# A planner's prices for transposes, single-precision products and scans are set anew

## The chip, the cores and the metric

The kernel runs on one core of a Trainium2 chip. The metric is the device time of one execution in microseconds (us). PE is the matrix engine, PEld its weight loads, DVE the vector engine, ACT the scalar engine, SP the engine that issues most DMAs, POOL a general engine that does almost nothing here. PE accumulates into eight banks of PSUM; all other tiles lie in SBUF.

## The reference

A trunk of two layers on one sequence of 512 tokens with 1024 features, in float32. Each layer is a half-step SwiGLU feed-forward block, a mixer, and another feed-forward block, every one behind an RMSNorm and added to `x`; a last RMSNorm ends it.

```python
for i in range(DEPTH):                        # DEPTH = 2
    x = x + 0.5 * swiglu(rmsnorm(x, ffn1_norm[i]), ...)    # 1024 -> 2816 -> 1024
    h = rmsnorm(x, mix_norm[i])
    y = gla_mixer(h, ...) if i % 2 == 0 else sb_mixer(h, ...)
    x = x + y
    x = x + 0.5 * swiglu(rmsnorm(x, ffn2_norm[i]), ...)
return rmsnorm(x, final_norm)

# gla_mixer: four heads, q and k of 128, v of 256; b = cumulative log decay
scores[t, s] = sum_k q[t, k] * exp(b[t, k] - b[s, k]) * k[s, k]      # s <= t
state = exp(b_last) * state + (k * exp(b_last - b)).T @ v
o = rmsnorm(scores @ v + (q * exp(b)) @ state) * silu(g);  y = o @ w_out

# sb_mixer: sixteen heads of 64; mask is s < t
z = q @ k.T / 8
sp = where(mask, softplus(z), 0)
rem = reverse_cumsum(sp) - sp
w = where(mask, exp(log_sigmoid(z) - rem), 0);  y = (w @ v) @ w_out
```

## The kernel before

`x` is kept transposed, as eight tiles of 128 features by 512 tokens. Large products are made in three: weight and operand are each split into a high part, rounded by ACT (`wh`, `xh`, `oh`, a CAST), and a low part, the remainder that DVE takes (`wl`, `xl`, `ol`, a subtraction); PE then forms high by high, low by high and high by low (line 475, `mm`). Weights arrive by DMA in pieces of 128 by 1024 numbers (`raw`) and are split in lines 534 and 535. Work inside the mixers that is not a weight product stays in plain single precision on PE: transposes against `ident`, products of weights with values.

The program has six stages: feed-forward; the gated linear attention (GLA), about 343 to 547 us; feed-forward twice; the stick-breaking mixer (SB), about 1199 to 1422; feed-forward.

In GLA the heads follow one another; while PE projects for later parts (`ps_f`, `ps_t`), a head's output is formed. The names used below: `osq`, the squares of the head's output (ACT, DVE line 1641); `sh` and `sl`, the split of their sum (`sl` by DVE, line 1648); `ps_on`, two products that sum `sh` and `sl` over the features; `y`, the scale made of it (line 1658); `gn`, the gate (line 1413 to 1423); `kd`, the decayed keys of the next head (DVE lines 1580 and 1587), transposed on PE in line 1597 (`ps_kd`). `ps_s` is the update of the state (line 1607).

In SB a step `s` treats one of the 16 heads in three groups of query blocks. The logits `ps_z` come from PE (line 1815, `kh`, `kl` and `mq` being the split keys and queries, `negm` the causal mask, which may be put in ahead and then opens the bank). ACT makes `l` = log(1 + exp(-abs z)) and `r` = relu(z) of it (lines 1857, 1032, 1860); DVE scans `l` + `r` backwards along the keys (line 1863, four scans a head of 512, 384, 256 and 128 numbers a partition), and subtracts the result from `ps_z` (line 1871), which frees the bank. A step later PE transposes that (`ps_T`, line 1885), ACT takes exp of it (`wt`, line 1032), and PE multiplies with the values for a pair of heads (`ps_oT`, line 1900), which is split into `oh` and `ol` (lines 1909, 1910). Beside it run the projections of the next heads (`ps_f`, evacuated as `n` by DVE in lines 1774 and 1792, then split and laid out by ACT and DVE in lines 1782 to 1802), and at the end of the stage the output projection (`ps_b`).

What order these instructions have on each engine is not that of the program's text. The program is written down once in an order; then `Planner` reads all its instructions and their dependences (`gather`), gives each a price in nanoseconds (`price`: when its result is there, `cost`, and for PE how long the engine is taken, `step`), works back from PE's instructions in the order of the text when each other instruction is due (`due`, `late`), and plays the program through (`run`). PE takes the first instruction of the text, among the next sixty open ones, that could start by now; the others take, of what is ready, the one due earliest, and may wait a little for one that is more urgent. SP goes by due times too. The resulting order of each engine's queue is then fixed. So a price is never a time on the chip: it changes which instruction stands ahead of which in a queue, and the semaphores between the engines stay.

The classes of price are told by the instruction's types and shapes. A scan was to be told by the name of the instruction's class:

```python
if "Scan" in kind:
    n *= 2
elif len(reads) == 1 and not psum_in and n > 256:
```

In this program the scan of line 1863 is an instruction of the class of SCALAR_TENSOR_TENSOR, so the first branch was never taken.

Of the kernel before, what the change touches and what calls it, by code (L numbers as in the profile page):

```python
# [19 lines left out]
P = 128  # L20
# [15 lines left out]
def spots(dims):  # L36

    m = 1
    for step, n in reversed(dims):
        if step == 1 and m == 1:  # L40
            m = (1 << n) - 1
        elif step:
            one = m
            for i in range(1, n):
                m |= one << (i * step)
    return m


class Planner:
# [31 lines left out]
    def gather(self):  # L81
        self.eng, self.ins, self.succ, self.pred, self.after, self.tiles = [], [], [], [], [], []
        self.held, self.cost, self.step = [], [], []
        tag = {t.name: str(t.cap_key() if callable(t.cap_key) else t.cap_key) for t in self.tc.info.tiles}
        pools = {p.id: p for p in self.tc.info.pools}
        self.bufs, self.pool_of = {}, {}
        for c in set(tag.values()):
            nm, _, pid = c.rsplit("_", 2)
            self.bufs[c] = pools[int(pid)].tag_meta[nm].bufs or 1
            self.pool_of[c] = int(pid)  # L90
        self.tag, self.users, self.first, self.index = tag, {}, {}, {}
        live, last_pe, bounds, masks = {}, {}, [], {}
        for i in self.bb.instructions:
            kind = type(i).__name__
            if kind.startswith("BassTile"):
                if kind == "BassTilePoolBoundary":
                    bounds.append((i.name, str(i.op), len(self.eng)))
                continue
            e = str(i.engine).split(".")[-1]
            k = self.index[i.name] = self.node(e, i)  # L100
            sizes, psum_in, wide = [], False, 0
            for write, refs in ((False, i.ins), (True, i.outs)):
                for r in refs:
                    b = getattr(r, "bass_ap", None)
                    if b is None:
                        continue
                    ap = [(int(s), int(n)) for s, n in b.ap]
                    n = 1
                    for _, c in ap[1:]:
                        n *= c  # L110
                    sizes.append((write, n, str(r.dtype), ap[0][1]))
                    t = b.tensor
                    if type(t).__name__ != "Tile" or t.name not in tag:
                        continue
                    bank = "pp" in tag[t.name].rsplit("_", 2)[1]
                    psum_in |= bank and not write
                    free = 1
                    for d in t.shape[1:]:
                        free *= int(d)
                    if bank:  # L120
                        m = 1
                    else:
                        key = (free, int(b.offset), tuple(ap))
                        m = masks.get(key)
                        if m is None:
                            at = int(b.offset) + sum(s * (n - 1) for s, n in ap[1:] if s < 0)
                            one = spots([(abs(s), n) for s, n in ap[1:]]) << (at % free)
                            p0, m = at // free // 32, 0
                            for q in range(p0, p0 + (ap[0][1] + 31) // 32):
                                m |= one << (q * free)  # L130
                            masks[key] = m
                    if t.name not in self.first:
                        self.first[t.name] = k
                        self.users[t.name] = []
                        live[t.name] = ([], [])
                    if not self.users[t.name] or self.users[t.name][-1] != k:
                        self.users[t.name].append(k)
                        self.tiles[k].append(t.name)
                    writes, reads = live[t.name]
                    for x, mx in writes:  # L140
                        if x != k and mx & m and not (bank and e == "PE" == self.eng[x]):
                            self.edge(x, k)
                    if write:
                        for x, mx in reads:
                            if x != k and mx & m:
                                self.edge(x, k)
                        writes[:] = [(x, mx & ~m) for x, mx in writes if mx & ~m] + [(k, m)]
                        reads[:] = [(x, mx & ~m) for x, mx in reads if x == k or mx & ~m]
                        if bank and e == "PE":
                            if last_pe.get(t.name, k) != k:  # L150
                                self.order(last_pe[t.name], k)
                            last_pe[t.name] = k
                    else:
                        if bank:
                            for x, _ in reads:
                                if x != k and self.eng[x] != e:
                                    self.edge(x, k)
                        reads.append((k, m))
            self.cost[k], self.step[k] = self.price(i, kind, e, sizes, psum_in)
        self.n_ins = len(self.eng)  # L160
        for a, b in self.behind_:
            self.order(self.index[a], self.index[b])
        self.seq = {}
        for t in sorted(self.first, key=lambda t: (self.first[t], int(t.rsplit("_", 1)[1]))):
            self.seq.setdefault(tag[t], []).append(t)
        self.place = {t: j for l in self.seq.values() for j, t in enumerate(l)}
        self.at = [float(k) for k in range(self.n_ins)]
        self.stack(bounds, pools)
        self.tables()

    def price(self, i, kind, e, sizes, psum_in):
        n = max((s[1] for s in sizes), default=1)
        if e == "PE":
            types = [s[2] for s in sizes]
            if any("bfloat16" in t for t in types):
                return 270.0, max(64.0, 0.43 * n)
            if any("float32r" in t for t in types):
                return 165.0 + 0.42 * n, max(112.0, 0.422 * n)
            moving = sizes[0][1]
            full = sizes[1][1] == P and not kind.endswith("Transpose") and not getattr(i, "is_transpose", False)  # L180
            return 150.0 + 0.9 * n, max(58.0, 0.845 * moving) * (2 if full and moving in (1, P) else 1)
        if "DMA" in kind:
            total = max((s[1] * s[3] for s in sizes), default=1) * 4
            return 2050.0 + total / 318.0, total / 318.0
        scalars = sum(1 for s in sizes[:-1] if s[1] == 1 and n > 1)
        if e == "DVE":
            reads = [s for s in sizes[:-1] if s[1] > 1]
            if "Scan" in kind:
                n *= 2
            elif len(reads) == 1 and not psum_in and n > 256:  # L190
                n *= 0.5
            return 148.0 + 1.045 * n + 60.0 * scalars, 0.0
        if e == "Activation":
            if "Load" in kind:
                return 1290.0, 0.0
            return 190.0 + 0.835 * n + 95.0 * scalars - 30.0 * psum_in, 0.0
        return 200.0 + n, 0.0
# [2129 lines left out]
```

## Time and profile before

| | us |
|---|---|
| median of three runs | 1750.26 (1749.68 to 1750.9) |
| profiled execution | 1753.55 |
| its span | 1751.6 |
| PE busy | 1741.9 |
| PE weight loads busy | 1630.5 |
| DVE busy | 1586.3 |
| ACT busy | 1078.2 |
| scans (line 1863), 16 each of 512, 384, 256, 128 | 19.6, 15.3, 10.9, 6.4 |
| transposes in SB (line 1885), 160 | 22.8 |
| state products in GLA (line 1607), 24 records | 6.5 |

How to read the rows: an instruction's row in the timeline gives its start from the span's start, its duration, engine, line, operation, `out<-in` and shapes; in square brackets stands how long the engine was idle before it, and what ended that. PE's products are pipelined and overlap, so how fast PE goes is seen from the distance of two starts, not from the durations. A plain single-precision product has two records (the 12 state products have 24). A window's row gives start and end, its length, and for each engine busy time and count.

### The profile page before, as it was taken

The page shows a single profiled execution, that of the slowest core. Times are in us where ns is not written, and L with a number is a line of the kernel's source. Part 1 is how long each engine was busy: PE and PEld are TensorE (multiplying, and loading weights), DVE is VectorE, ACT ScalarE, POOL GpSimd, SP SyncE. Part 2 cuts the span into 40 slices and gives each one's busy share as a digit, 9 for nine tenths or more (in the row PEclk, how much of TensorE's full clock was granted, in tenths as well). Part 3 has the DMA queues.
Part 4 walks back from the last instruction along what each step waited for, and adds up shares of the span by engine and source line. Part 5 has one row for each costly group of instructions (what it writes and reads, how often), then busy time and mean ns, then how long its engine had stood idle before and what let it go on. Part 6 is the DMA issues. An engine that isn't in the chain of part 4 may idle for free.

```text
span 1751.6 us, 31640 instructions
## 1 busy us (share of the span) xinstructions
PE 1741.9 (99%) x12810; PEld 1630.5 (93%) x12810; DVE 1586.3 (91%) x2688; ACT 1078.2 (62%) x1898; POOL 9.9 (1%) x24
## 2 busy tenths in 40 slices
PE   9999999999999999999999999999999999999998
PEld 8999999888888999999989999999888889999997
DVE  8999999787888989999899999996898679999996
ACT  7556566554656565565655566566888755665655
POOL 0000000100000000000000000000000000000000
PEclk9999999999999999999999999999999999999999
DMA  6333333321223333333323333332222233333422
GB/s 190 125 98 120 97 122 121 106 70 53 73 97 97 121 116 102 97 121 113 126 77 119 99 107 121 109 103 79 61 73 73 73 97 121 121 97 104 130 93 73
DMA packets 176710, 179.27 MB, mean 102 GB/s; under 512 B 4082, under 2 KB 166180, under 8 KB 176564
## 3 DMA queue, kind: packets, MB, share of 16 engines
q1 hardware_dynamic: 175712, 175.91, 32.1%
q8 instruction: 100, 1.64, 0.4%
q0 software_dynamic: 608, 1.05, 0.2%
q14 instruction: 46, 0.38, 0.1%
q10 hardware_dynamic: 244, 0.29, 0.0%
HBM read 175.17 MB, written 2.10 MB: 101 GB/s over the span
## 4 chain that ended last, share of the span: by engine, by line
PE 85%; DVE 11%; ACT 1%; issue 1%; DMA 1%; DVEq 0%
PE ps_w L1134 18%; PE ps_f L475 17%; PE ps_d L475 10%; PE ps_q L1134 9%; PE ps_w L812 5%; PE ps_t L475 5%; PE ps_b L475 5%; PE ps_z L1134 5%; DVE wl L535 4%; PE ps_q L812 3%; DVE x L818 1%; PE ps_z L812 1%; PE ps_z L1815 1%; DMA rawd<-in_ffn_w_down_dram 1%; PE ps_S L475 1%
## 5 line engine op out<-in xcount | busy, mean ns | idle before, releaser
L535 DVE TENSOR_TENSOR wl<-raw,wh 128x1024 fp32r<-128x1024 f32 x241 | 256.5, 1066 | 42.0 <-ACT wh L534 41.4
L534 ACT CAST wh<-s 128x1024 fp32r<-128x1024 f32 x192 | 201.7, 1051 | 148.1 <-DVE s L1126 41.5
L534 ACT CAST wh<-raw 128x1024 fp32r<-128x1024 f32 x241 | 221.6, 921 | 78.6 <-PE ps_f L475 33.6
L1134 PE MATMUL ps_w<-th,wh 128*128 128x256 f32 x864 | 238.2, 276 | 0.2
L1134 PE MATMUL ps_w<-tl,wh 128*128 128x256 f32 x864 | 237.7, 275 | 0.0
L1134 PE MATMUL ps_w<-th,wl 128*128 128x256 f32 x864 | 237.7, 275 | 0.0
L535 DVE TENSOR_TENSOR wl<-s,wh 128x1024 fp32r<-128x1024 f32 x192 | 235.2, 1226 | 2.7 <-ACT wh L534 2.6
L475 PE MATMUL ps_f<-xh,wh 128*128 128x512 f32 x432 | 166.8, 386 | 0.0
L1134 PEld LDWEIGHTS ps_w<-th,wh 128*128 128x128 f32 x864 | 166.0, 192 | 0.7 <-ACT o L1167 0.7
L1134 PEld LDWEIGHTS ps_w<-tl,wh 128*128 128x128 f32 x864 | 166.0, 192 | 0.0
L1134 PEld LDWEIGHTS ps_w<-th,wl 128*128 128x128 f32 x864 | 166.0, 192 | 0.0
L475 PE MATMUL ps_f<-xl,wh 128*128 128x512 f32 x432 | 163.8, 379 | 0.0
L475 PE MATMUL ps_f<-xh,wl 128*128 128x512 f32 x432 | 163.8, 379 | 0.0
L475 PE MATMUL ps_d<-hh,wh 128*128 128x512 f32 x288 | 109.4, 380 | 0.0
L475 PE MATMUL ps_d<-hl,wh 128*128 128x512 f32 x288 | 109.3, 380 | 0.0
L475 PE MATMUL ps_d<-hh,wl 128*128 128x512 f32 x288 | 109.2, 379 | 0.0
L535 DVE TENSOR_TENSOR wl<-rawd,wh 128x512 fp32r<-128x512 f32 (+1 forms) x108 | 93.0, 867 | 1.4 <-ACT wh L534 1.4
L534 ACT CAST wh<-rawd 128x512 fp32r<-128x512 f32 (+1 forms) x108 | 80.6, 764 | 21.0 <-PE ps_d L475 12.0
L475 PEld LDWEIGHTS ps_f<-xl,wh 128*128 128x128 f32 x432 | 81.7, 189 | 11.5
L475 PEld LDWEIGHTS ps_f<-xh,wh 128*128 128x128 f32 x432 | 81.8, 189 | 11.0
L475 PEld LDWEIGHTS ps_f<-xh,wl 128*128 128x128 f32 x432 | 81.8, 189 | 10.7
L1134 PE MATMUL ps_q<-th,wh 128*128 128x256 f32 x288 | 79.3, 275 | 0.0
(349 smaller groups left out, 5506.1 us busy)
## 6 DMA issues: line engine op xcount, KB each, us to landing
raw<-in_ffn_w_gate_dram SPq DMA_DIRECT2D x43, 1024.0 KB, 5.4
raw<-in_ffn_w_up_dram SPq DMA_DIRECT2D x43, 1024.0 KB, 5.3
rawd<-in_ffn_w_down_dram SPq DMA_DIRECT2D x84, 512.0 KB, 3.5
raw<-in_gla_w_in_dram SPq DMA_DIRECT2D x12, 1024.0 KB, 5.2
raw<-in_sb_w_in_dram SPq DMA_DIRECT2D x16, 512.0 KB, 3.8
raw<-in_gla_w_out_dram SPq DMA_DIRECT2D x4, 1024.0 KB, 5.0
raw<-in_sb_w_in_dram SPq DMA_DIRECT2D x4, 1024.0 KB, 5.1
raw<-in_sb_w_out_dram SPq DMA_DIRECT2D x4, 1024.0 KB, 5.1
```

The lines of the kernel that those rows point to most:

```text
L475: nc.tensor.matmul(ps, l, r, start=first, stop=last)
L534: nc.scalar.copy(h[:, k], part)
L535: nc.vector.tensor_tensor(out=l[:, k], in0=part, in1=h[:, k].bitcast(F32), op=ALU.subtract)
L812: st["pe"] = nc.tensor.matmul(ps, l_, r_, start=first and c + n == 0, stop=c == 1 and n == 2, skip_group_check=True).ins
L818: nc.vector.scalar_tensor_tensor(out=x, in0=ps, scalar=0.5, in1=x, op0=ALU.mult, op1=ALU.add)
L1134: st["pe"] = nc.tensor.matmul(o, l_, r_, start=first and j + n == 0, stop=j == 3 and n == 2, skip_group_check=True).ins
L1815: nc.tensor.matmul(o_, l_, r_, start=first, stop=last, skip_group_check=True)
```

## The change

`gather` notes of each instruction whether one of its access patterns runs backwards (a negative step), and hands that to `price` as `scan`; the unused `wide` goes. `price` doubles a DVE instruction's length where `scan` is set. On PE, transposes, single-precision products with 128 weight columns, and the rest of the plain products each get a formula of their own. Nothing in the computation is touched. The lines behind the edit are four further down (1863 is 1867 after).

```diff
-            sizes, psum_in, wide = [], False, 0
+            sizes, psum_in, scan = [], False, False
...
                     ap = [(int(s), int(n)) for s, n in b.ap]
+                    scan |= any(s < 0 for s, _ in ap)
...
-            self.cost[k], self.step[k] = self.price(i, kind, e, sizes, psum_in)
+            self.cost[k], self.step[k] = self.price(i, kind, e, sizes, psum_in, scan)
...
-    def price(self, i, kind, e, sizes, psum_in):
+    def price(self, i, kind, e, sizes, psum_in, scan):
...
             moving = sizes[0][1]
-            full = sizes[1][1] == P and not kind.endswith("Transpose") and not getattr(i, "is_transpose", False)
-            return 150.0 + 0.9 * n, max(58.0, 0.845 * moving) * (2 if full and moving in (1, P) else 1)
+            if i.is_transpose:
+                return 273.0, 109.0
+            if sizes[1][1] == P:
+                return max(362.0, 180.0 + 1.62 * moving), max(200.0, 1.7 * moving)
+            return 172.0 + 0.86 * moving, max(60.0, 0.85 * moving)
...
-            if "Scan" in kind:
+            if scan:
                 n *= 2
```

In the planner's prices, in nanoseconds: scans of 512, 384, 256 and 128 go from 683, 549, 416 and 282 to 1218, 951, 683 and 416; the state products of line 1607 take PE 435 instead of 216; a transpose is 273 and takes 109, instead of 265 and 108; products of 128 by 128 have their result after 387 instead of 265 and take 218 instead of 216.

All instructions stay, each on its engine. The queues of SP and POOL are as before. The queues of PE, ACT and DVE differ in 18, 35 and 114 places, all of them in GLA and SB; the feed-forward stages are as before. Three places follow.

**SB, DVE, around 1344 us.** `n_15985` is the scaled query tile of a pair of heads, which ACT then casts into the `mq` of its two heads; `l_15952` and `r_15951` belong to the 512-wide scan of a head in work, whose subtract frees the bank `ps_z_15947`. Before:

```order
L1802 CAST kl_15906<-kl_15906 64x512
L1863 SCALAR_TENSOR_TENSOR l_15952<-r_15951,l_15952 128x512
L1871 TENSOR_TENSOR r_15951<-ps_z_15947,l_15952 128x512
L1774 SCALAR_TENSOR_TENSOR n_15985<-ps_f_15934,R_14405 128x512
L535 TENSOR_TENSOR wl_16298<-raw_15737,wh_16297 128x1024
L1783 TENSOR_TENSOR mq_16015<-n_15985,mq_16015 64x512
L1863 SCALAR_TENSOR_TENSOR l_16008<-r_16007,l_16008 128x384
```

After:

```order
L1806 CAST kl_15906<-kl_15906 64x512
L1778 SCALAR_TENSOR_TENSOR n_15985<-ps_f_15934,R_14405 128x512
L1867 SCALAR_TENSOR_TENSOR l_15952<-r_15951,l_15952 128x512
L1787 TENSOR_TENSOR mq_16015<-n_15985,mq_16015 64x512
L1875 TENSOR_TENSOR r_15951<-ps_z_15947,l_15952 128x512
L539 TENSOR_TENSOR wl_16298<-raw_15737,wh_16297 128x1024
L1787 TENSOR_TENSOR mq_16018<-n_15985,mq_16018 64x512
L1867 SCALAR_TENSOR_TENSOR l_16008<-r_16007,l_16008 128x384
```

`n` and the first `mq` now stand ahead of work that they stood behind: `n` ahead of scan and subtract, `mq_16015` ahead of the subtract.

**SB, PE, around 1384 us.** `ps_b` are banks of the output projection; `oh` and `ol` are the two parts of the heads' outputs. Before:

```order
L475 MATMUL ps_b_16317<-ol_16124,wh_16305 128x512
L475 MATMUL ps_b_16448<-oh_14899,wh_16297 128x512
L475 MATMUL ps_b_16448<-oh_14899,wl_16298 128x512
L475 MATMUL ps_b_16448<-ol_14900,wh_16297 128x512
L475 MATMUL ps_b_16452<-oh_14899,wh_16297 128x512
```

After:

```order
L479 MATMUL ps_b_16317<-ol_16124,wh_16305 128x512
L479 MATMUL ps_b_16313<-oh_16383,wh_16309 128x512
L479 MATMUL ps_b_16313<-oh_16383,wl_16310 128x512
L479 MATMUL ps_b_16313<-ol_16384,wh_16309 128x512
L479 MATMUL ps_b_16448<-oh_14899,wh_16297 128x512
L479 MATMUL ps_b_16448<-oh_14899,wl_16298 128x512
L479 MATMUL ps_b_16448<-ol_14900,wh_16297 128x512
```

Three products into the bank `ps_b_16313`, which is open already, stand ahead of the first one into the new bank `ps_b_16448`.

**GLA, third head, around 494 us.** On DVE, before:

```order
L1423 TENSOR_TENSOR gn_5670<-gn_5670,sg_5672 128x512
L1641 SCALAR_TENSOR_TENSOR osq_5743<-osq_5743,osq_5806 128x512
L1423 TENSOR_TENSOR gn_5726<-gn_5726,sg_5728 128x512
L1648 TENSOR_TENSOR sl_5810<-osq_5743,sh_5809 128x512
L1580 TENSOR_TENSOR kd_5848<-b_4754 128x384
L1413 TENSOR_TENSOR gn_5825<-ps_f_5785,R_4383 128x512
L535 TENSOR_TENSOR wl_5912<-raw_5529,wh_5911 128x1024
```

After:

```order
L1427 TENSOR_TENSOR gn_5670<-gn_5670,sg_5672 128x512
L539 TENSOR_TENSOR wl_5912<-raw_5529,wh_5911 128x1024
L1645 SCALAR_TENSOR_TENSOR osq_5743<-osq_5743,osq_5806 128x512
L1427 TENSOR_TENSOR gn_5726<-gn_5726,sg_5728 128x512
L1652 TENSOR_TENSOR sl_5810<-osq_5743,sh_5809 128x512
L1584 TENSOR_TENSOR kd_5848<-b_4754 128x384
L1417 TENSOR_TENSOR gn_5825<-ps_f_5785,R_4383 128x512
```

The low part of a weight piece, `wl_5912`, stands five places earlier, ahead of `osq` and `sl`. On PE the second `ps_on` product, which reads `sl`, stood right behind the first one; now three `ps_f` products of a projection stand between them (in the first two heads one `ps_t` product does).

## The prediction

> **What bounds the kernel now.** First the page's busy times, then the windows by stage, then the starts on PE.
>
> ```profile
> span 1751.6 us, 31640 instructions
> PE 1741.9 (99%) x12810; PEld 1630.5 (93%) x12810; DVE 1586.3 (91%) x2688; ACT 1078.2 (62%) x1898; POOL 9.9 (1%) x24
> ...
> core 0: us, PE busy (x) PEld busy (x) DVE busy (x) ACT busy (x) POOL busy (x), PEclk, DMA share, GB/s
> 343.00:547.00 204.00, 203.99 (x1417) 178.97 (x1418) 164.90 (x307) 113.07 (x178) 0.31 (x1) 1.00 0.23 73
> 1199.00:1422.00 223.00, 221.97 (x1387) 188.44 (x1387) 174.81 (x257) 174.87 (x342) 0.00 (x0) 1.00 0.24 74
> ```
>
> PE is without work for 1751.6 − 1741.9 = 9.7 us. In the gated-linear-attention stage (GLA, the window from 343) it is 204.00 − 203.99 = 0.01, in the stick-breaking stage (SB, from 1199) 223.00 − 221.97 = 1.03; the other 8.7 lie elsewhere. The order of the queues differs only inside GLA and SB, so those 8.7 us and the feed-forward stages are out of its reach.
>
> Busy is not the same as going at its pace, so I read starts against starts. [...]
>
> ```profile
> 22.86 31.28 PE ps_f L475 x144
> ...
> L475 PEld LDWEIGHTS ps_f<-xh,wh 128*128 128x128 f32 x432 | 81.8, 189 | 11.0
> ```
>
> 31.28 / 144 = 0.217 us from start to start. What can be won are places where the next start comes later than that. I went through GLA and SB for them; the view of PE's waits names two in SB:
>
> ```profile
> PE ps_oT L1900 <- ACT wt L1032: 0.7, 1, 0.7
> PE ps_b L475 <- DVE r L1871: 0.3, 1, 0.3
> ```
>
> **The change part by part.** No operation is added or removed. Prices alone change, and through them the order. The price that moves most is the scan's, which was booked at little over half of what it takes: 683 ns where the first row below shows 1.23 us.
>
> *SB, 1344 to 1358.* Here ACT comes late with the last exponential (`wt`), and PE waits in the middle of its value products:
>
> ```profile
> 1343.47 1.23 DVE L1863 TENSOR_TENSOR_SCAN l<-r,l 128x512 f32<-128x512 f32 x1
> ...
> 1345.41 0.68 DVE L1774 SCALAR_TENSOR_TENSOR n<-ps_f,R 128x512 f32<-128x512 f32 x1
> ...
> 1346.12 0.62 ACT L1782 CAST mq<-n 64x512 fp32r<-64x512 f32 x1 [2.25 <-DVE n L1774]
> ...
> 1346.12:1356.56 10.44, 10.32 (x21) 1.00 0.01 3
> ...
> 1354.47 1.04 ACT L534 CAST wh<-raw 128x1024 fp32r<-128x1024 f32 x1
> 1356.18 0.38 ACT L1032 ACTIVATE wt<-ps_T 128x256 f32<-128x256 f32 x1
> ...
> 1343.90 0.34 PE L1815 MATMUL ps_z<-negm,idb 128*128 128x128 bf16 x2
> 1347.71 0.39 PE L1815 MATMUL ps_z<-kh,mq 128*128 128x512 f32 x1
> 1353.73 2.15 PE L1900 MATMUL ps_oT<-wt,w 128*64 128x512 f32 x10
> 1356.62 0.86 PE L1900 MATMUL ps_oT<-wt,w 128*64 128x256 f32 x6 [0.74 <-ACT wt L1032]
> 1357.41 0.44 PE L1815 MATMUL ps_z<-kh,mq 128*128 128x384 f32 x1
> ...
> 1375.70 0.34 PE L1815 MATMUL ps_z<-negm,idb 128*128 128x128 bf16 x2
> 1376.19 2.38 PE L1900 MATMUL ps_oT<-wt,w 128*64 128x512 f32 x16
> 1378.49 0.45 PE L1815 MATMUL ps_z<-kh,mq 128*128 128x384 f32 x1
> ```
>
> The value products took 1357.41 − 1353.73 = 3.68 us here and 1378.49 − 1376.19 = 2.30 two groups later: **1.38 lost** (0.74 shown as idle, the rest hidden in the modelled ends). ACT had idled 2.25 us for `n` and then worked without a break until that `wt` ended: 10.32 of 10.44 us, by the window between them. The change puts `n` ahead of scan and subtract. The products that `n` reads are early: six others stand between the last of them and the pair of mask products at 1343.90 (L1815 from `negm`, which opens the banks of the next head), 6 × 0.217 = 1.3 us. So `n` would start where the scan did, 1343.47, and end at 1344.15 instead of 1346.09, and ACT's chain may run 1.9 us earlier. Behind `n` the scan, and by another 0.68 the subtract, are late: the subtract ends about 1346.8 instead of 1345.5. Its bank is wanted at 1347.71, so PE hides that. `wt` would end at 1356.56 − 1.9 = 1354.6. PE wants it when its ten products are through: in the undisturbed group all sixteen take 2.30, and the ten ahead, the wider ones, an estimated 1.6, until 1355.3. The cover is 0.7 us. I take the loss as gone: **−1.38**. From both sides: if something else holds up ACT's chain, for which nothing speaks but the cast at 1354.47 that needs its weights, the gain is 0; the whole is 1.38.
>
> *SB, 1384.* A product of the output projection waits for a bank that the subtract frees:
>
> ```profile
> 1383.86 0.38 PE L475 MATMUL ps_b<-ol,wh 128*128 128x512 f32 x1
> 1384.53 0.48 PE L475 MATMUL ps_b<-oh,wh 128*128 128x512 f32 x1 [0.29 <-DVE r L1871]
> 1384.85 0.38 PE L475 MATMUL ps_b<-oh,wl 128*128 128x512 f32 x1
> ...
> 1379.23 0.69 DVE L1910 TENSOR_TENSOR ol<-ps_oT,oh 128x512 fp32r<-128x512 f32 x1 [0.60 <-ACT oh L1909]
> 1383.92 0.56 DVE L1871 TENSOR_TENSOR r<-ps_z,l 128x384 f32<-128x384 f32 x1
> ```
>
> 1384.85 − 1383.86 = 0.99 for two starts against 2 × 0.217: **0.55 lost**. The change puts three products ahead of the waiting one. Their operands are ready at 1379.92, their bank was in use already, and they fill 3 × 0.217 = 0.65 us, more than the loss: **−0.55**, if the subtract stays where it is. If it also ends later by a scan of the two that took 1.00 us (next fence), the wait comes back: bounds −0.55 and 1.00 − 0.65 = +0.35.
>
> *SB, the subtracts.* In seven places of SB (the heads between 1263 and 1373) the first subtract of a head, which frees a bank, goes behind two scans that now look long. They took 1.00 us together; with the steps between, the subtract ends 1.0 to 1.1 later. The first and the tightest place:
>
> ```profile
> 1263.64 0.56 DVE L1871 TENSOR_TENSOR r<-ps_z,l 128x384 f32<-128x384 f32 x1
> 1264.11 1.00 DVE L1863 TENSOR_TENSOR_SCAN l<-r,l 128x256 f32<-128x256 f32 x2
> 1269.70 0.34 PE L1815 MATMUL ps_z<-negm,idb 128*128 128x128 bf16 x2
> ...
> L1871 DVE TENSOR_TENSOR r<-ps_z,l x3: 558/559/692, 1372.4 to 1377.9; 128x384 f32<-128x384 f32 x2, 128x512 f32<-128x512 f32 x1
> ```
>
> The mask pair takes the bank 1269.70 − 1264.20 = 5.5 us after the first subtract ends, and 1375.70 − (1372.4 + 0.56) = 2.7 after the last: the work that hides the move is PE's products between, and it covers 1.1 everywhere. Cost 0 with that cover, 0.55 a place (the wait just seen) without it. I book +0.3 for half of one such wait somewhere; bounds 0 and 1.4.
>
> *GLA, heads 1 to 3.* The second product of the head's norm (`ps_on`) waits for DVE's `sl`:
>
> ```profile
> 422.93 0.38 PE L475 MATMUL ps_on<-sh,one 128*128 128x512 f32 x1
> 423.29 0.48 PE L475 MATMUL ps_on<-sl,one 128*128 128x512 f32 x1
> 423.61 0.38 PE L475 MATMUL ps_t<-wh,xh 128*128 128x512 f32 x1
> ...
> 494.07 0.69 DVE L1648 TENSOR_TENSOR sl<-osq,sh 128x512 fp32r<-128x512 f32 x1
> 495.74 2.35 DVE L535 TENSOR_TENSOR wl<-raw,wh 128x1024 fp32r<-128x1024 f32 x2
> 494.81 0.48 PE L475 MATMUL ps_on<-sl,one 128*128 128x512 f32 x1
> 501.98 0.56 DVE L1587 TENSOR_TENSOR kd<-kd,k 128x384 f32<-128x384 f32 x1
> 502.69 0.52 PE L1597 MATMUL ps_kd<-ident,kd 128*128 128x128 f32 x3
> ```
>
> 423.61 − 422.93 = 0.68 against 0.43: 0.25 lost a head. With one product between (0.217), heads 1 and 2 win it back: **−0.5** (bounds 0 and −0.5). In the third head three products go between, but DVE takes a weight split (`wl`, 2.35 / 2 = 1.18) ahead. `sl` then ends near 494.76 + 1.18 = 495.94, or 495.75 if short gaps ahead of it close by 0.2, as I allow. The product starts at 494.81 now, of which, by head 1's rows, 0.36 − 0.217 = 0.14 is wait; it would be reached at 494.81 − 0.14 + 0.65 = 495.3. It waits about 0.4 and loses 0.1 at the restart, in place of the 0.25 lost now: +0.25. Behind it `kd` comes later while the transposes that read it are placed one product (0.217) earlier; `kd` now ends at 502.54 and they start at 502.69, so the cover is 0.15; I add 0.35 for it, a third of what it would be if `kd` came late by the whole 1.18. Together **+0.6**; bounds −0.25 (`sl` in time) and +0.25 + 1.18 + 0.22 − 0.15 = +1.5.
>
> **Sum** on the profiled execution: −1.38 − 0.55 + 0.3 − 0.5 + 0.6 = −1.5. Its own time is 1753.55, 3.3 above the median 1750.26 of the three runs; carried over as a difference, 1750.26 − 1.5 = **1748.7**. The bounds added up are −1.38 − 0.55 − 0.5 − 0.25 = −2.7 and 0.35 + 1.4 + 1.5 = +3.3, each of which would need all at once.
>
> **The rivals.**
>
> *The stages have more room than waits show.* PEld is busy 178.97 of 204 us in GLA and 188.44 of 223 in SB, against 93% overall; a better order that brought both to 93% would save 204 − 178.97 / 0.93 = 11.6 and 223 − 188.44 / 0.93 = 20.4 us. Against it: a stream of 512-wide products at full pace has its loads busy for 189 / 217 = 87%, about where GLA's 88% and SB's 84.5% stand already. Time, for a fifth of the 32 us: 1750.3 − 6.4 = 1743.9. [...]
>
> *Slower: the subtracts hold banks too long.* Place: SB, the mask pair or projection that opens a bank behind a postponed subtract. Price 0.55 each; it decides against the kernel by over 0.2% from about ten places on: 10 × 0.55 = 5.5, less the 1.05 of GLA's heads and of 1384, gives 1750.3 + 4.5 = 1754.8. Against it stand the 2.7 and more of cover.
>
> *The gains are taken back.* The late `wt` stays or another re-forms (+1.4), and GLA's third head reaches its bound (1.5 − 0.6 = 0.9 on top): 1748.7 + 2.3 = 1751.0, no change. For it speaks that the cast of 1.04 us at 1354.47 stands in ACT's queue two places ahead of that `wt`; against it the 0.7 of cover.
>
> *It does nothing.* The queues differ but no start that PE waits for moves: 1750.3. The two waits listed are 1.0 us in all, which speaks for it.
>
> **How the numbers follow.** A measurement here tells about 0.2%, 3.5 us, from no change: below 1746.8 is faster, above 1753.8 slower. My forecast, a gain of 0.5 to 3, gets 0.58; gains taken back 0.20; nothing 0.15; more room 0.03; subtracts 0.04. Faster is 0.03, same 0.93, slower 0.04. The range 1747.0 to 1751.2 goes from the forecast with its one doubtful price, GLA's third head, near its good bound and the others in full (1748.7 − 0.85 − 0.3 = 1747.5, and 0.5 for the scatter of the median) to the rival that takes the gains back.
>
> **What would show it.** In the trace after, right: no wait for `wt` at 1356 and value products in 2.3 us there; three projection products ahead of the one that waited at 1384, and no wait there; two `ps_on` starts 0.43 apart in heads 1 and 2. Wrong: PE waiting for `r` at more than two places in SB, for `sl` or `kd` over 1 us in GLA, or any difference in the feed-forward stages.

## The result, and the profile after

The changed kernel takes 1747.73 us, median of 20 runs (1747.31 to 1749.38); the kernel before, on the same chip and in as many runs, 1750.45 (1749.68 to 1752.3). The ratio is 0.9984, 95% interval 0.9978 to 0.9991: 2.7 us less, between 1.6 and 3.9. That is clear of zero, though within the 0.2% that the prediction called no change. The time lies in the range 1747.0 to 1751.2, 1.0 under the forecast 1748.7. One of the ten executions of the kernel with two moves on DVE, below, took 3020.09 us and is left out of its median; why is not known.

The page after, its busy times and one of PE's waits:

```profile
span 1745.8 us, 31640 instructions
PE 1736.7 (99%) x12810; PEld 1627.3 (93%) x12810; DVE 1583.9 (91%) x2688; ACT 1079.6 (62%) x1898; POOL 9.9 (1%) x24
...
PE ps_on L479 <- ACT sh L1651: 0.3, 1, 0.3
```

The view of PE's waits names five; the other four lie outside GLA and SB. The two waits of the stick-breaking stage (SB), for `wt` and for `r`, are gone. One is new: in GLA, for ACT's `sh`.

The span fell by 5.8 us, more than twice what the runs show. So the profiles must be cut by stage before they are compared. PE's queue has the same number of places in both kernels; the stages begin and end at places where both have the same product. The same four places of PE's timeline, first of before, then of after: second product of `ps_gk` and a first `ps_f` product behind GLA (1087 places on), a second `ps_t` product ahead of SB and a `ps_f` product behind it (1318 places on).

```profile
343.27 0.38 PE L475 MATMUL ps_gk<-xl,gs 128*128 128x512 f32 x1
547.07 0.38 PE L475 MATMUL ps_f<-xh,wh 128*128 128x512 f32 x1
1199.02 0.28 PE L475 MATMUL ps_t<-wl,xh 128*128 128x256 f32 x1
1422.16 0.38 PE L475 MATMUL ps_f<-xh,wh 128*128 128x512 f32 x1
```

```profile
341.51 0.38 PE L479 MATMUL ps_gk<-xl,gs 128*128 128x512 f32 x1
545.33 0.38 PE L479 MATMUL ps_f<-xh,wh 128*128 128x512 f32 x1
1195.54 0.28 PE L479 MATMUL ps_t<-wl,xh 128*128 128x256 f32 x1
1416.64 0.38 PE L479 MATMUL ps_f<-xh,wh 128*128 128x512 f32 x1
```

SB took 1422.16 − 1199.02 = 223.14 us and takes 1416.64 − 1195.54 = 221.10: **−2.04**. GLA took 547.07 − 343.27 = 203.80 and takes 545.33 − 341.51 = 203.82: **+0.02**. Measured in the same way from four profiles (the first column goes from PE's first row to its 44th):

| profile | first 11 us | GLA | feed-forward 547 to 1188 | SB | feed-forward behind SB |
|---|---|---|---|---|---|
| before | 11.17 | 203.80 | 641.02 | 223.14 | 322.38 |
| before, again | 9.56 | 203.81 | 638.71 | 223.15 | 322.68 |
| changed | 9.40 | 203.82 | 639.27 | 221.10 | 322.15 |
| changed, again | 9.56 | 203.81 | 638.64 | 221.10 | 322.17 |

In GLA and SB two executions of one kernel agree within 0.02 us, and profiles of different kernels with the same order in GLA within 0.07 there; that is a far finer measure than the time of a run. In the other three columns the queues are the same, and yet the second profile of before is 1.6 and 2.3 us under the first in two of them. So the 3.8 of the 5.8 us of span that lie outside GLA and SB are no more than two executions of one kernel differ by. What the change did in the stages that it touches is −2.0.

The places of the prediction, after. SB around 1350, on DVE, ACT and PE:

```profile
1339.45 0.69 DVE L1778 SCALAR_TENSOR_TENSOR n<-ps_f,R 128x512 f32<-128x512 f32 x1
...
1340.36 1.26 ACT L1786 CAST mq<-n 64x512 fp32r<-64x512 f32 x2
1350.42 0.38 ACT L1036 ACTIVATE wt<-ps_T 128x256 f32<-128x256 f32 x1
...
1350.12 2.37 PE L1904 MATMUL ps_oT<-wt,w 128*64 128x512 f32 x16
1352.42 0.45 PE L1819 MATMUL ps_z<-kh,mq 128*128 128x384 f32 x1
```

`wt` ends at 1350.80, 0.68 after PE began the value products; before it ended 1356.56 − 1353.73 = 2.83 after. The products take 1352.42 − 1350.12 = 2.30 in place of 3.68.

GLA's norm, on PE, in the first and in the third head, and ACT's `sh` in the third:

```profile
421.16 0.38 PE L479 MATMUL ps_on<-sh,one 128*128 128x512 f32 x1
421.38 0.38 PE L479 MATMUL ps_t<-wh,xh 128*128 128x512 f32 x1
421.59 0.42 PE L479 MATMUL ps_on<-sl,one 128*128 128x512 f32 x1
421.85 0.38 PE L479 MATMUL ps_t<-wl,xh 128*128 128x512 f32 x1
...
492.03 0.38 PE L479 MATMUL ps_f<-xl,wh 128*128 128x512 f32 x1
492.71 0.48 PE L479 MATMUL ps_on<-sh,one 128*128 128x512 f32 x1 [0.30 <-ACT sh L1651]
...
492.04 0.62 ACT L1651 CAST sh<-osq 128x512 fp32r<-128x512 f32 x1 [1.22 <-DVE osq L1645]
```

In the first head three starts follow at 0.22, 0.21 and 0.26 us: of the 0.25 lost, 0.21 are won. In the third head PE comes to `ps_on` 492.71 − 492.03 − 0.217 = 0.46 late, since `sh` ends at 492.66.

### The profile page after: what moved, and what is told of

Read it like the earlier page. It is cut to its first block, busy times and chain, and to the rows that moved or that the text cites. A ratio compares the mean times of both kernels' runs of the same rounds, so it can differ in the third digit from the quotient of the medians.

```text
span 1745.8 us, 31640 instructions
## 1 busy us (share of the span) xinstructions
PE 1736.7 (99%) x12810; PEld 1627.3 (93%) x12810; DVE 1583.9 (91%) x2688; ACT 1079.6 (62%) x1898; POOL 9.9 (1%) x24
## 4 chain that ended last, share of the span: by engine, by line
PE 91%; DVE 7%; issue 1%; DMA 1%; ACT 0%; SPq 0%; DVEq 0%; ACTq 0%
PE ps_w L1138 20%; PE ps_f L479 18%; PE ps_d L479 11%; PE ps_q L1138 10%; PE ps_w L816 6%; PE ps_z L1138 5%; PE ps_t L479 5%; PE ps_b L479 5%; PE ps_q L816 3%; DVE wl L539 2%; PE ps_z L816 2%; PE ps_z L1819 2%; PE ps_oT L1904 1%; PE ps_T L1889 1%; PE ps_bt L479 1%; DVE x L822 1%
```

## The experiments

All times are medians beside the kernel before on the same chip; the stage times are by starts on PE, as above. Three kernels (before once more, the three products alone, the weight split put back) ran once, for their profile. "Moves" are moves of single instructions in the finished queue of an engine; nothing else differs then.

**The kernel before, once more.**

> The kernel before, once more, for a second profile. Between the two profiles shown 5.8 us lie, but the places that the change reaches account for 2.0 of them (SB -1.94, GLA -0.05 by starts on PE); 1.69 come in the first 11 us, where the products of the first profile stood 0.43 us apart until 10.3 us and those of the changed kernel only until about 5 us, and 1.8 in the feed-forward stages between 547 and 1188 us, where both kernels have the same queues. Theory A: these 3.5 us are scatter between executions; the second profile of the same kernel differs from the first by a us or two in just these two stretches, and by less than 0.1 in GLA and SB. Rival B: they belong to the order (the changed kernel meets another rhythm of transfers after GLA): then this profile repeats the first within 0.3 us everywhere.

The profile is the second row of the table above: 1.61 and 2.31 us less than the first in the two stretches that were named, GLA and SB within 0.02. Theory A holds. The first profile of before was a high one, and so the sum of the prediction, made on it as a difference, was carried over rightly, but a span compared with a span would have told 5.8.

**One class of prices at a time.**

```diff
-            if i.is_transpose: ...  if sizes[1][1] == P: ...      # scans alone
+            full = ...                                            # PE as before
```

```diff
-            if scan:                                              # PE alone
+            if "Scan" in kind:
```

> The changed kernel with the old prices on PE, so that the scans alone are priced anew. Queues differ from those before in SB only. Theory A (the gain is SB's: the late wt at 1356 and the bank at 1384): SB is 1.9 us shorter by starts on PE, GLA is as before; time about 1.9 us under before, that is 0 to 0.2 us from the full change. Rival B (the gain comes from GLA's transposes and state products or from something between the two): less than half of it, 1.0 or less.

> The changed kernel with scans priced as before, so that PE's products and transposes alone are priced anew. Queues differ in GLA only. Theory A: heads 1 and 2 win 0.21 each at the norm's second product, head 3 loses 0.46 + 0.10 at its first product (ACT's square sum is late, since DVE took a weight split ahead) and 0.14 at the transposes, against 0.25 won; in all -0.05 by starts on PE, time within 0.3 us of before. Rival B: GLA's order carries the gain, -1 us or more.

| | time | ratio to before | GLA | SB |
|---|---|---|---|---|
| scans alone | 1748.29 | 0.9988 (0.9979 to 0.9996) | 203.78 | 221.22 |
| PE alone | 1750.19 | 0.9998 (0.9989 to 1.0006) | 203.85 | 223.17 |
| before | 1750.52 | | 203.81 | 223.15 |

The scans' price alone gives SB its −1.9 and leaves GLA; PE's prices alone leave SB's times and give GLA +0.04, no more than the scatter there. Theory A holds for both. The halves do not quite add up, though: with the scans priced anew, PE's prices also turn PE's order in SB, between 1380 and 1393 us, and SB is 221.10 with both against 221.20 to 221.22 in the three kernels with the scans alone. That is another 0.1.

**Two moves on DVE.**

```diff
+ DVE: n_15985 (L1774) ahead of the scan l_15952; mq_16015 (L1783) ahead of the subtract r_15951
```

> The kernel before with two moves on DVE and nothing else: the query tile n at 1345.4 goes ahead of the 512-wide scan and its subtract, and the first low part mq made of it ahead of the subtract. Theory A (n made ACT's chain late, and that made wt late): n ends at 1344.15, no wait for wt at 1356, the value products there take 2.30 instead of 3.68, the time falls by 1.38 us and nothing else changes. Rival B (ACT's chain is held up by its weight cast or by the scans, so moving n alone is not enough): the products still take over 3.0 us, gain under 0.7.

SB took 221.65, 1.49 less; the time was 1748.27, median of nine, ratio 0.9989 (0.9979 to 0.9998). The place, on DVE and PE, and the waits:

```profile
1339.56 0.69 DVE L1777 SCALAR_TENSOR_TENSOR n<-ps_f,R 128x512 f32<-128x512 f32 x1
...
1349.20 0.34 PE L1818 MATMUL ps_z<-negm,idb 128*128 128x128 bf16 x2
1349.37 0.38 PE L1888 MATMUL ps_T<-ident,r 128*128 128x128 f32 x2
1349.68 1.72 PE L1903 MATMUL ps_oT<-wt,w 128*64 128x512 f32 x8
1351.99 0.45 PE L1818 MATMUL ps_z<-kh,mq 128*128 128x384 f32 x1
...
PE ps_b L478 <- DVE r L1874: 0.3, 1, 0.3
```

The value products take 1351.99 − 1349.68 = 2.31, and the wait for `wt` is gone, while that for `r` stays. The 0.11 beyond the expected 1.38 lies at the two mask products (L1818), which stand 1349.37 − 1349.20 = 0.17 ahead of the transposes here and stood 0.31 ahead before. Two moves, where the queue of DVE alone differs in 114 places, give three quarters of SB's gain. Theory A holds.

**Three products on PE, and then three more.**

```diff
+ PE: ps_b_16313<-oh_16383 (three products) ahead of the first product into ps_b_16448
```

> The kernel before with one move on PE: the three products into the open bank that the change puts ahead at 1383 (1393 in the old order). Theory A: they fill 0.65 us, the wait of 0.45 for the subtract and the restart of 0.10 go, SB is 0.55 us shorter. Rival B (the bank's wait moves on, since the subtracts behind it are late too): gain 0.2 or less.

SB took 223.14: no gain at all. PE's timeline in this kernel, at the place and 11 us on:

```profile
1380.25 0.38 PE L478 MATMUL ps_b<-oh,wh 128*128 128x512 f32 x1
1380.47 0.38 PE L478 MATMUL ps_b<-oh,wl 128*128 128x512 f32 x1
...
1391.78 0.48 PE L478 MATMUL ps_b<-oh,wh 128*128 128x512 f32 x1
1392.53 0.48 PE L478 MATMUL ps_b<-oh,wh 128*128 128x512 f32 x1 [0.27 <-ACT oh L1912]
1392.85 0.59 PE L478 MATMUL ps_b<-oh,wl 128*128 128x512 f32 x2
```

The wait at the first place is gone, as expected. But the three products had themselves been a filler: in the old order they stood between the last value products and the first product that reads what ACT makes of these, `oh` of the last pair. With them gone PE comes there 1392.85 − 1391.78 − 0.43 = 0.64 too early. Rival B named the wrong wait, yet its number is the right one. The next kernel puts other products into that hole, as the change does, and has the two moves on DVE too.

```diff
+ DVE: as above;  PE: as above, and ps_b_16317<-oh_16383 (two products) and
+      ps_b_16448<-oh_16383 (one) ahead of the first product that reads oh_16519
```

> The kernel before with the two moves of n and mq on DVE at 1344 us, the three products put ahead at 1383, and three more moved at 1396: two products of the open bank ps_b_16317 and one of ps_b_16448 go ahead of the first product that reads the last pair's oh, as in the changed kernel. Eleven instructions move or are passed over in place of the hundred and more that the new scan price moves. Theory A (the gain of SB is these few): n gives 1.49, and the three products give 0.55 once the hole that they leave at 1392 is filled: SB 2.04 shorter, the same as with the whole change. Rival B (the other moves on DVE and ACT carry a part): 1.5 to 1.8.

SB took 221.28, 1.86 less; the time 1747.59 (before: 1750.19; ratio 0.9986, 0.9977 to 0.9995). Eight moves give 1.86 of 2.04, a little more than rival B's 1.5 to 1.8. Yet its reason does not hold. Start for start, SB in this kernel and in the changed one part by 0.18 at a single place:

```profile
1390.79 0.69 DVE L1916 TENSOR_TENSOR ol<-ps_oT,oh 128x512 fp32r<-128x512 f32 x1 [0.85 <-ACT oh L1915]
...
1391.54 0.48 PE L481 MATMUL ps_b<-ol,wh 128*128 128x512 f32 x1
1391.86 0.38 PE L481 MATMUL ps_b<-oh,wh 128*128 128x512 f32 x1
```

The product that reads the last pair's `ol` (ready at 1391.48) comes 0.08 late, and the next one 0.10 later than its pace; in the changed kernel two more products stand ahead of it. So the 0.18 belongs to PE's order there, and the other moves on DVE and ACT, the late subtracts among them, cost and gain nothing in SB: Theory A holds but for one hole left.

**What a late subtract costs.** The change puts subtracts that free a bank of `ps_z` behind scans. To see the price, eleven of them are put back further:

```diff
+ DVE: the second subtract (L1875) of eleven heads behind the next 512-wide scan
```

```diff
+ DVE: the same eleven, behind the subtract that follows that scan
```

> The changed kernel with the second subtract of eleven heads (1261 to 1369 us) put further back on DVE, behind the next 512-wide scan: it ends 2.2 to 3.9 us later than it did. In the changed kernel the bank that it frees was taken 1.7 to 4.4 us after its end. Theory A (a late subtract costs only what is over its cover): seven places lose 0.4, 1.1, 0.7, 0.4, 1.3, 0.5 and 1.0 us, with 0.1 for each restart 6.0 us in all; four places lose nothing. Rival B (the price of a place is the 0.55 once seen): 11 x 0.55 = 6.0 too, but spread evenly, over all eleven. Rival C (PE's products in between are free to run on, no cost): under 1 us.

> The same eleven subtracts, one step further back, behind the subtract that follows that scan: they end 3.4 to 5.3 us later. Theory A (over its cover): all eleven places lose, 0.1 to 2.7 us each, 17.7 in all and 1.1 for the restarts: 18.8 us slower than the changed kernel. Rival B (a fixed price): 6.0 again. Rival C: under 1 us.

SB took 225.69 and 235.03, against 221.10: +4.59 and +13.93. The times were 1753.47 (ratio to before 1.0016, 1.0007 to 1.0025) and 1763.32 (1.0070, 1.0056 to 1.0083). PE's waits in the first kernel, summed; then the fourth head on PE and on DVE, where the subtract ends at 1301.82 and the mask product that needs its bank starts at 1301.88:

```profile
PE ps_z L1822 <- DVE r L1878: 3.5, 6, 1.0
...
1301.88 0.28 PE L1822 MATMUL ps_z<-negm,idb 128*128 128x256 bf16 x1 [0.96 <-DVE r L1878]
...
1301.29 0.53 DVE L1878 TENSOR_TENSOR r<-ps_z,l 128x384 f32<-128x384 f32 x1
```

The place lost against what was expected, head by head in order of time (delay less cover):

| | 1 | 2 | 3 | 4 | 5 | 6 | 7 | 8 | 9 | 10 | 11 |
|---|---|---|---|---|---|---|---|---|---|---|---|
| behind the scan, expected | 0 | 0 | 0.42 | 1.11 | 0.66 | 0 | 0.36 | 1.28 | 0.48 | 0 | 1.03 |
| measured | 0 | 0 | 0.44 | 1.12 | 0.09 | 0 | 0.37 | 1.16 | 0.36 | 0 | 1.03 |
| behind the subtract, expected | 0.09 | 1.41 | 2.14 | 2.39 | 1.46 | 0.52 | 2.07 | 2.72 | 1.65 | 0.47 | 2.74 |
| measured | 0 | 0.96 | 1.67 | 1.95 | 0.43 | 0.07 | 1.62 | 2.15 | 1.09 | 0 | 2.30 |

Theory A holds in the first at ten places of eleven: the price is the delay less the cover, not a fixed 0.55, and a place with cover pays nothing. The fifth pays 0.09 in place of 0.66: there the scan that was let pass starts 0.57 earlier, since the subtract itself (0.55) had kept DVE from it. The 0.1 for a restart does not occur at these places.

In the second kernel each place that pays comes out 0.44 to 0.57 under what was expected, the fifth 1.03. The fourth place there, on DVE and PE:

```profile
1304.11 0.68 DVE L1878 TENSOR_TENSOR r<-ps_z,l 128x512 f32<-128x512 f32 x1
1304.71 0.54 DVE L1878 TENSOR_TENSOR r<-ps_z,l 128x384 f32<-128x384 f32 x1
...
1304.84 0.28 PE L1822 MATMUL ps_z<-negm,idb 128*128 128x256 bf16 x1 [1.78 <-DVE r L1878]
```

PE goes on 0.05 after the end of the 512-wide subtract (1304.79), and the one that was moved ends only at 1305.25. It is so at all eight places where PE waits: it went by the subtract that now ends first, and I had counted to the end of the other, 0.46 later. That the mask product now opens the bank which the first one frees would fit; the trace does not tell the banks apart. The second kernel also shows something else, below.

**GLA's third head.**

```diff
+ DVE, with PE's prices alone: wl_5912 (L535) behind gn_5825 again, as before the change
```

> The kernel with PE's new prices alone, with one move on DVE taken back: in GLA's third head the low part of the weight piece (wl_5912) stands behind gn_5825 again, as before. It tells what the loss of 0.46 + 0.10 at the first ps_on product was. Theory A (the weight split made the sum of squares late, and behind it the chain on DVE to kd is the bound): the wait at the first ps_on product goes, but kd ends when it ended, since the same work lies on DVE ahead of it, so that PE now waits for it 0.4 to 0.5 longer at ps_kd; GLA within 0.15 of where it was. Rival B (only the split was in the way): GLA 0.45 to 0.56 shorter than with PE's prices alone.

GLA took 204.21: 0.36 longer than with PE's prices alone, although the wait at `ps_on` went:

```profile
492.13 0.48 PE L482 MATMUL ps_on<-sh,one 128*128 128x512 f32 x1
...
501.06 0.52 PE L1604 MATMUL ps_kd<-ident,kd 128*128 128x128 f32 x3 [0.89 <-DVE kd L1594]
...
490.73 0.69 DVE L1648 SCALAR_TENSOR_TENSOR osq<-osq 128x512 f32<-128x512 f32 x1 [0.58 <-ACT osq L1644]
500.36 0.55 DVE L1594 TENSOR_TENSOR kd<-kd,k 128x384 f32<-128x384 f32 x1
```

PE is at `ps_on` 0.47 earlier and then loses 0.91 at `kd` (another 0.09 is won at 373 us, where the order is the same). What bounds this head is the work on DVE up to `kd`, and that work is the same in both kernels: the split stands ahead of `kd` either way. But counted from the start of GLA, `kd` ends at 159.46 here and at 159.11 with the split in front, 0.35 later, and that is the loss. DVE idles 0.58 for ACT's part of `osq` now; with PE's prices alone the split had filled that hole, and `osq` followed without a wait. Theory A has the right bound; its "kd ends when it ended", and with it "within 0.15", was wrong by this hole.

**Two versions meant to beat both.** Scans priced anew, GLA's order as before, and

```diff
+ PE, heads 1 to 3: two projection products between the two ps_on products
```

```diff
+ the same, and DVE, head 3: kd (L1587) ahead of on (L1665, twice) and on times gn (L1673, twice)
```

> A version meant to join the gains: scans priced anew (SB as in the changed kernel), GLA's order as before, but with two projection products put between the two products of the norm in the first three heads. Theory A: SB -1.94; in GLA 0.25 a head, -0.75 in all; together 2.7 us under before and 0.7 under the changed kernel. Rival B (the products that are moved make the next wait): GLA as before or slower, time as in the changed kernel.

> A version meant to beat both: scans priced anew, GLA's order as before but with two products between the two ps_on products in three heads, and in the third head kd on DVE ahead of the four instructions that finish the head (on, twice, and on times gn, twice). Theory A (what the two products won was lost again at kd): the 0.25 lost at ps_kd goes, GLA is 0.75 to 0.8 shorter than before, SB 1.94; 2.7 us under before, 0.7 under the changed kernel. Rival B (the head's output is late instead, since on moves back by 0.47): GLA 0.5 shorter, as without this move.

> The changed kernel once more, beside the joined version on the same chip. GLA and SB by starts on PE within 0.05 of its first profile; the first 11 us and the stages between 547 and 1188 us anywhere within the 2 us that executions have differed by there. The time 2.0 to 2.7 us under before.

| | time | ratio to before | GLA | SB | feed-forward behind SB |
|---|---|---|---|---|---|
| two products between | 1747.88 | 0.9986 (0.9977 to 0.9995) | 203.27 | 221.20 | 322.77 |
| and kd ahead | 1747.85 | 0.9987 (0.9978 to 0.9996) | 203.21 | 221.21 | 322.94 |
| changed, again | 1747.59 | 0.9987 (0.9978 to 0.9996) | 203.81 | 221.10 | 322.17 |

In the first, three times 0.25 is won at the norms and 0.25 lost at `ps_kd`: the next wait that rival B feared took a third of it. PE there, in the first and in the second version:

```profile
500.30 0.38 PE L479 MATMUL ps_b<-oh,wl 128*128 128x512 f32 x1
500.76 0.52 PE L1601 MATMUL ps_kd<-ident,kd 128*128 128x128 f32 x3
```

```profile
499.99 0.38 PE L482 MATMUL ps_b<-oh,wl 128*128 128x512 f32 x1
500.20 0.49 PE L1604 MATMUL ps_kd<-ident,kd 128*128 128x128 f32 x3
```

0.46 from start to start becomes 0.21: that loss is gone, though 0.17 come back at the products just behind it. GLA is 0.6 shorter than in the changed kernel. The time does not show it: both versions stand within 0.3 us of the changed kernel, well inside their intervals. Part of that can be read: the feed-forward behind SB was 0.6 and 0.8 us longer in these profiles, by starts on PE mostly at one place each: 0.35 behind a wait for `x` in the first, 0.5 behind one for `hl` in the second. A wait for `hl` is shown with the scans alone too (0.5) and in the second profile of before (0.2), and in others with the same queue there it is not. What sets these waits stays open. So neither version is shown to beat the change.

## Why the prediction was right

Right were the sign, roughly the size (1.5 forecast; 2.0 by stages, 2.7 by the runs), and that the feed-forward stages have no part in it. The signs named for "right" came: no wait for `wt`, 2.3 us of value products, no wait at 1384, and `ps_on` starts 0.43 apart in heads 1 and 2. By its own steps:

- **SB, 1344 to 1358 (−1.38).** As worked out: `n` ahead of the scan alone takes the wait for `wt` away, 1.49 with the mask pair. The cover was there, and larger: `wt` ends at 1350.80, and the eleventh product, which had waited for it, starts 1.77 behind the first (estimated 1.6), at 1351.89; that is 1.1 in place of 0.7.
- **SB, 1384 (−0.55).** The sum was right, the step was not whole. The full change wins 0.55 there, but the three products named win nothing alone; they leave a hole of 0.64 at the last pair's `oh`. I had asked whether their operands were ready at the new place, and not what they had covered at the old one. That the change moves other products into that hole was luck for this term: the prediction did not know of the hole.
- **SB, the subtracts (+0.3).** They cost 0: the cover was as read, the kernel with eight moves, which leaves these places as they were, gains nothing over the change, and the two kernels with late subtracts show that the cover is what counts. The rival "slower" had the wrong price: a place pays nothing until its cover (1.7 to 4.4 us for the eleven that were moved) is used up.
- **GLA, heads 1 and 2 (−0.5).** 0.21 each, −0.42; of the 0.25, 0.04 come back at the start behind the second `ps_on`.
- **GLA, head 3 (+0.6).** In all +0.45, near the forecast by luck, for most of it lies at another instruction: not `sl` but `sh` was late, since the weight split stands ahead of `osq`, which ACT's `sh` reads. That is 0.46 and 0.10 at the restart, and 0.14 at `ps_kd`, less the 0.25 won at `sl`. The late `kd` was named; that it decides over all else in this head was not.
- **The sum (−1.5).** Term by term the profiles give −2.04 + 0.02 = −2.0. The 0.5 between is mostly the 0.3 booked for the subtracts and 0.1 each for the mask pair and the third head. The runs show −2.7, with −1.6 to −3.9 as the interval; in the last set 1747.59 against 1750.19, −2.6. The 0.6 beyond −2.0 is inside that interval and not explained. Other kernels' medians stand off their stage times by like amounts, both ways: 0.7 lower with the eight moves, 0.4 higher in the first kernel with late subtracts.
- **The rivals.** "More room" did not come: the loads of PE were 93% busy before and are after, and the gain is that of the named waits. The gains were not taken back, and the change did do what it says, but half of it (PE's prices) is worth nothing alone and 0.1 beside the scans.

## What to carry to other kernels

A planner's price is worth what the few instructions are worth whose place it turns: here a scan booked at half put one query tile behind it, and that one tile was three quarters of the gain, while the repriced products of PE alone gained nothing. Before a filler is moved into a hole, ask which hole it fills now (the three products at 1384 and the weight split in GLA both left one behind); before a freed bank is called late, subtract its cover. And gains of a microsecond are seen by starts on the bounding engine, stage by stage between like instructions; the spans of two executions of the same kernel differed here by 3.6 us (1751.6 and 1748.0).

## What had not been expected of the hardware

PE fell to half its pace once in the middle of a kernel. In the second kernel with late subtracts, behind a wait of 1.99 us, PE's timeline and windows read:

```profile
1350.92 0.28 PE L1822 MATMUL ps_z<-negm,idb 128*128 128x256 bf16 x1 [1.99 <-DVE r L1878]
1352.33 0.63 PE L482 MATMUL ps_f<-xh,wh 128*128 128x512 f32 x1
1352.75 0.63 PE L482 MATMUL ps_f<-xh,wl 128*128 128x512 f32 x1
...
1352.00:1355.40 3.40, 3.40 (x11) 2.83 (x11) 1.71 (x3) 3.11 (x8) 0.00 (x0) 0.53 0.01 2
```

Products of 512 columns start 0.42 apart in place of 0.217 (31.28 us for 144 of them, before), and the granted clock is 0.53 for 3.4 us and 1.00 in the window behind (1355.4 to 1360); by starts that costs another 1.7 us, nearly as much as the wait itself. The length of a wait alone does not decide it: a longer one in the same kernel, 2.13 us at 1386, was not followed by this (granted clock 1.00 from 1386.3 to 1392). The start of the kernel has the same two paces. Before, in its first and in its second profile:

```profile
7.72 0.63 PE L2117 MATMUL ps_f<-xh,wh 128*128 128x512 f32 x1
8.15 0.63 PE L2117 MATMUL ps_f<-xh,wl 128*128 128x512 f32 x1
```

```profile
7.68 0.38 PE L2117 MATMUL ps_f<-xh,wl 128*128 128x512 f32 x1
7.89 0.38 PE L2117 MATMUL ps_f<-xl,wh 128*128 128x512 f32 x1
```

0.43 against 0.21 in the same program. Of the fourteen profiles three ran the first 11 us so (11.12 to 11.17), the other eleven in 9.30 to 9.78; the three are 1.3 to 1.9 us longer. The traces' records of the granted clock begin, with 1.00, 10.4 us into the span in the first profile of before and 4.6 us into it in the changed kernel's, where 512-wide products start 0.22 apart from 7.27 on. What sets that time is not shown, nor why the wait of 1.99 us was followed by the half pace and that of 2.13 was not. All this is read off single executions; no run varied it.
